# Hybrid attention block on Trainium2: branch B's output projection in strips of 256 columns with six banks for the heads, and rotary blocks whose squares have no fixed order

## The chip, the cores and the metric

The kernel runs on one core of one Trainium2 chip. The metric is the device time of one execution in microseconds. The engines are TensorE (PE; its weight loads are listed apart as PEld), VectorE (DVE), ScalarE (ACT), GpSimd (POOL) and SyncE (SP), which issues every DMA of this kernel in one queue, in order. PSUM has eight banks of 128 x 512 float32.

## The reference, cut to what matters

One layer of an encoder block over 512 tokens of width 2048, in float32:

```python
h = rmsnorm(x, norm_g)
qa, ka, va, za, qb, kb, vb, zb, ga, gb = split(h @ w_in)        # w_in: 2048 x 10752
# branch A: differential attention, 8 heads of 128 (two halves of 64)
qa, ka = apply_rope(qa), apply_rope(ka)
p  = softmax(q1 k1^T / 8) - lam * softmax(q2 k2^T / 8)
oa = rmsnorm(p @ va, subln_g) * (1 - lam_init)
ya = (oa * silu(za)) @ w_out_a                                  # 1024 x 2048
# branch B: 8 query heads, 2 key heads of 128, normalised, then axial rotary
qb = axial_rope(rmsnorm(qb, q_norm_g)); kb = axial_rope(rmsnorm(kb, k_norm_g))
ob = softmax(qb kb^T / sqrt(128)) @ vb
yb = (ob * silu(zb)) @ w_out_b                                  # 1024 x 2048
merged = sigmoid(ga) * ya + sigmoid(gb) * yb
out = rmsnorm(x + merged @ w_o, final_g)
```

## The kernel before

**Products in parts.** Each float32 operand of a large product is written as hi + lo, both in the type fp32r: `hi_lo` casts on ScalarE (L115, `w_hi<-w_raw`) and subtracts on VectorE (L116, `w_lo<-w_raw,w_hi`). Three matmuls (hi hi, hi lo, lo hi) then stand for one. Weights come in tiles of 128 x 1024 numbers (`w_raw`), eight buffers; the split tiles `w_hi`, `w_lo` have three buffers each. So the two splits of a tile run ahead of TensorE by at most two or three tiles.

**Stages.** The input is normalised and turned; then come the projections of `w_in`. The large ones use Strassen's scheme, seven products for eight (`strassen`, L197 on, whose matmuls of 256 columns are L248; the wide form has L329). The last Strassen stage is the four projections of the gates z (L654 to L667): each is a call of `strassen` with 336 matmuls of 256 columns, 24 to a weight tile. Its results pass `gate`, a SiLU on ScalarE (L659) and a store (L661). After each call some blocks of branch B's queries and keys get their norm and rotary factors.

**A rotary block** is `rope_b` (L606 to L634): a load of 128 x 512 from the scratch `pv` into `cols` (L612), four squares with row sums on ScalarE (L617), a reciprocal root on GpSimd (L111, L112 in `rsqrt_pool`), four products and sums on GpSimd (L628 twice, L629, L630), for the two key heads (numbers 8 and 9) four scalings on ScalarE (L633), and a store to `pv` (L634). `tc.keep_in_program_order` holds the squares where the program has them in ScalarE's queue. The list `to_rope` says which blocks are written behind which of the four projections. In the text below the blocks are called R1 to R10 in the order of that list: 0, 8, 1, 2, ...

**Who orders what.** A scheduler orders the instructions of every engine. In the attention stage TensorE alone follows the program's order by hand (`manual_schedule`), and the others follow the scheduler.

**Attention** has sixteen heads in the order `HEADS`: B0 B1 A0 B2 B3 A1 B4 B5 B6 A2 B7 A3 A4 A5 A6 A7. Each head makes four tiles of scores (an A head two products for each), takes the softmax, turns the four tiles of p (`turn_p`: four transposes into one bank, then the splits `ph` and `pl` out of it), and multiplies with v (`attend`, in `finish`). An A head ends with `norm`: a matmul with ones sums the squares `sqh`, `sql` of the output. PSUM banks come in two rings: `acc` for projections and `aux` for heads. Six of the eight banks are in `aux`, two in `acc`.

**Fillers.** While heads wait for their softmax, TensorE takes steps of other work: `fill(n)` takes n steps from the generator `fillers`. Each is one weight tile with its 24 or so matmuls. First come the last projections (`FILL_BLOCKS`), then, from the last A heads on, branch B's output projection yb. `FILLS` holds three digits for each head, the number of steps at its three places. In the projection, yb goes through four strips of 512 columns. A strip has four blocks of tokens at a time, so it takes four banks: before it starts, two banks go from `aux` to `acc`. When a bank is complete, `yb_done` loads the gate `gg`, multiplies on VectorE and stores to `yg`.

```python
ring = banks["aux"]
banks["acc"] += [ring.pop(0), ring.pop(0)]
...
few = len(banks["aux"]) < 6
```

So `few` is true from the head on in which yb begins, and then the turning of p is in two halves with a step between, and one step stands between the third and fourth tile of scores. The branch's head outputs are kept in SBUF or in the scratch `og` and split with `og_split` when a step needs them. After the heads come ya (L1057 on), the last product with `w_o`, and the final norm.

Of the kernel before, what the change touches and what calls it, by code (L numbers as in the profile page):

```python
# [11 lines left out]
F32 = mybir.dt.float32  # L12
F32R = mybir.dt.float32r
AF = mybir.ActivationFunctionType
ALU = mybir.AluOpType
AX = mybir.AxisListType

P = 128
D = 2048
S = 512  # L20
NT = S // P
# [30 lines left out]
def hybrid_block_kernel(  # L52
# [8 lines left out]
    nc = tc.nc  # L61
# [5 lines left out]
    banks = {}  # L67
# [10 lines left out]
    def share_banks(**kw):  # L78
        banks.update(kw)
# [10 lines left out]
    def aux(*shape):  # L90
        return bank("aux", shape or (S,))
# [284 lines left out]
    gg = dram.tile([S, 2 * D], F32, name="gg")  # L376
    og = dram.tile([2 * BW, S], F32, name="og")
    yg = dram.tile([S, D], F32, name="yg")
# [59 lines left out]
    with tc.tile_pool(name="xs", bufs=1) as xs:  # L438
# [4 lines left out]
        sq = xs.tile([P, D], F32, name="sq", tag="s4h")  # L443
        with tc.tile_pool(name="xn", bufs=1) as xn:
# [5 lines left out]
            for t in range(NT):  # L450
                for i in range(2):
                    c = slice(i * (D // 2), (i + 1) * (D // 2))
# [5 lines left out]
            ps = aux()  # L458
            nc.tensor.transpose(out=ps[:, :NK], in_=grow, identity=ident[:NK, :NK])
            nc.vector.tensor_copy(out=gn, in_=ps[:, :NK])  # L460
            for t in range(NT):
                ss = xn.tile([P, 2], F32, name="ss", tag="ss", bufs=4)
                for i in range(2):
                    c = slice(i * (D // 2), (i + 1) * (D // 2))
# [4 lines left out]
                for c in (slice(0, 512), slice(512, 1024)):  # L469
                    v = xt[:, t].rearrange("p (k c) -> p k c", k=2)[:, :, c]  # L470
# [105 lines left out]
        with tc.tile_pool(name="sp", bufs=6) as sp:  # L576
# [29 lines left out]
            def rope_b(n):  # L606


                b = B_QB + n if n < 8 else B_KB + n - 8
                assert written[b] == NT  # L610
                v = sp.tile([P, NT, P], F32, name="cols", tag="cols", bufs=2)
                nc.sync.dma_start(out=v, in_=pv[b])  # L612
                sq = sp.tile([P, P], F32, name="bsq", tag="bsq", bufs=1)
                ss = rb[:, n, :]
                for t in range(NT):
                    tc.keep_in_program_order(
                        nc.scalar.activation(out=sq, in_=v[:, t, :], func=AF.Square, accum_out=ss[:, t:t + 1]))  # L617
                if n < 8:

                    rsqrt_pool(ss, ss, 1.0, P * EPS, NT)  # L620
                else:
                    rsqrt_pool(ss, ss, 1.0 / P, EPS, NT)
                t2 = sp.tile([P, NT, P], F32, name="rope2", tag="rope2", bufs=1)
                tcb, tsb = tabs["q" if n < 8 else "k"]
                for r in range(2):
                    d, s, m = (x.rearrange("p t (a r j) -> p t a r j", r=2, j=32)[:, :, :, q, :]
                               for x, q in ((t2, r), (v, 1 - r), (tsb, r)))
                    nc.gpsimd.tensor_tensor(out=d, in0=s, in1=m, op=ALU.mult)  # L628
                nc.gpsimd.tensor_tensor(out=v, in0=v, in1=tcb, op=ALU.mult)  # L629
                nc.gpsimd.tensor_tensor(out=v, in0=v, in1=t2, op=ALU.add)  # L630
                if n >= 8:
                    for t in range(NT):
                        nc.scalar.mul(out=v[:, t, :], in_=v[:, t, :], mul=ss[:, t:t + 1])  # L633
                nc.sync.dma_start(out=pv[b], in_=v)  # L634

            b_table("q", q_norm_g)
            b_table("k", k_norm_g)
            to_rope = [(0, 8, 1), (2, 3, 4), (5, 9), (6, 7)]


            nc.sync.dma_start(out=sub_g, in_=subln_g.rearrange("o p -> p o"))
# [32 lines left out]
    at = ap.enter_context(tc.tile_pool(name="at", bufs=2))  # L674
# [221 lines left out]
    def og_tiles(half):  # L896
        ogq[half] = tuple(xa.tile([P, 8, S], F32R, name=f"og{half}{e}", tag=f"a{half + 1}{e}") for e in "hl")

    def og_act(k, t=None):
        return tuple(v[:, k % 8, :] if t is None else v[:, k % 8, t * P:t * P + P] for v in ogq[k // 8])  # L900
# [18 lines left out]
    def fill_steps(blocks, **kw):  # L919
        def place():  # L920
            return at.tile([P, S], F32, name="kq", tag="kq")

        return (plain_rows if blocks[0] < B_VA else plain_cols)(blocks, place, **kw)

    def fillers():
        for blocks in FILL_BLOCKS[:-1]:
            yield from fill_steps(blocks)

        for n, _ in enumerate(fill_steps(FILL_BLOCKS[-1], order=[8, 12, 0, 4])):
            if n == 3:  # L930
                og_tiles(1)
            og_split(3)
            yield
        og_tiles(0)

        ring = banks["aux"]
        banks["acc"] += [ring.pop(0), ring.pop(0)]
        for n in range(4):
            def yb_done(t, ps, n=n):
                rows = slice(t * P, (t + 1) * P)  # L940
                g = at.tile([P, S], F32, name="rows", tag="kq", bufs=2)
                nc.sync.dma_start(out=g, in_=gg[rows, D + n * S:D + n * S + S])
                nc.vector.tensor_tensor(out=g, in0=ps, in1=g, op=ALU.mult)
                nc.sync.dma_start(out=yg[rows, n * S:n * S + S], in_=g)

            steps = stream_steps(w_out_b, [(n * S, S)], 8, True, lambda k, t: og_act(8 + k, t), yb_done)
            for last in (10, 10, 12, 12, 14, 14, 16, 16):

                while not split_og.issuperset(range(8, last)):
                    og_split(1)  # L950
                    yield
                next(steps)
                og_split(1)
                yield

    filler = fillers()

    def fill(n):
        for _ in range(n):
            next(filler, None)  # L960


    with tc.manual_schedule(engines={mybir.EngineType.PE}):
        heads = [(HeadA if h[0] == "A" else HeadB)(int(h[1])) for h in HEADS]
        heads[0].prepare()
        heads[1].prepare()
        heads[0].double()
        fill(FILL_FIRST)
        heads[0].turn()
        fill(2)  # L970
        for n, head in enumerate(heads):
            f = [int(c) for c in FILLS[n]]
            last = heads[n - 1] if n else None
            if n + 1 < len(heads):
                heads[n + 1].double()
            few = len(banks["aux"]) < 6
            head.scores(0)
            head.scores(1)
            fill(f[0])
            if last:  # L980
                last.finish()
            head.scores(2)
            if few:
                fill(1)
            head.scores(3)
            if n + 1 < len(heads):
                heads[n + 1].turn()
            if n + 2 < len(heads):
                heads[n + 2].prepare()
            fill(f[1] - few)  # L990
            if few:
                head.turn_p((0, 1))
                fill(1)
                head.turn_p((2, 3))
            else:
                head.turn_p()
            if last:
                last.norm()
            fill(f[2] - few)
        head.finish()  # L1000
        head.norm()

# [2 lines left out]
        pass  # L1005
    og_split()
    ap.close()
    share_banks(acc=banks["acc"], aux=banks["aux"])


    mp = ctx.enter_context(tc.tile_pool(name="mp", bufs=1))
# [4 lines left out]
    with tc.tile_pool(name="ya", bufs=1) as yp:  # L1016
# [41 lines left out]
        for n in range(4):  # L1058
            rows = [None] * NT
# [9 lines left out]
            steps = stream_steps(w_out_a, [(n * 256, 256), (1024 + n * 256, 256)], 8, True, og_act, ya_done)  # L1069
# [192 lines left out]
```

## Time and profile before

| | before |
| --- | --- |
| device time, median of 3 runs | 1409.51 us (1408.02 to 1410.52) |
| the profiled execution | 1409.93 us |
| its span in the trace | 1408.2 us |
| mean granted clock of TensorE | 0.983 |
| PE busy | 1342.4 us, 95% of the span |
| PEld | 1180.6 us, 84% |
| DVE | 1079.7 us, 77% |
| ACT | 714.5 us, 51% |
| POOL | 224.1 us, 16% |

Busy times are those of one execution, taken by the profiler. Times in rows are microseconds from the start of the span, unless a row says ns. `out<-in` are the names of tiles in the program; a form such as 128x512 is partitions by elements. A granted clock of 1.0 is 2.4 GHz; it falls to 0.5, which is 1.2 GHz, and a number between is a mean over a stretch. The span ends 1.7 us below the execution's own time.

### The profile page before, as it was taken

How to read it: one execution, taken by the hardware profiler on the slowest of the kernel's cores; microseconds unless marked ns; L12 is line 12 of the kernel's file. 1: busy time of each engine (PE TensorE's matmuls, PEld its weight loads, DVE VectorE, ACT ScalarE, POOL GpSimd, SP SyncE). 2: the span in 40 equal slices, each digit the busy share in tenths (PEclk: the TensorE clock that was granted, in tenths of full speed). 3: DMA queues.
4: the chain of work that ended last, by engine and by line, in shares of the span. 5: the costliest groups of instructions: out<-in, count | busy, mean ns of one | idle time of the engine just before them, and what ended most of it. 6: DMA issues, size and time to landing. Idle time of an engine off the chain costs nothing. (4 is left out here: it accounts for less than half of the span.)

```text
span 1408.2 us, 20166 instructions
## 1 busy us (share of the span) xinstructions
PE 1342.4 (95%) x7625; PEld 1180.6 (84%) x7625; DVE 1079.7 (77%) x1271; ACT 714.5 (51%) x1104; POOL 224.1 (16%) x194
## 2 busy tenths in 40 slices
PE   6999999999999999989789899999899899999997
PEld 5998888888888888989789688888777778899997
DVE  5976877777787787868664587869888756799986
ACT  7643343444444444455344467657677643444444
POOL 1000000000000000543543411422220000004322
PEclk9999999999999999999899999999999999999999
DMA  8244654636372825535436684454554346453333
GB/s 284 81 146 134 201 173 133 211 97 232 91 253 75 269 90 179 166 112 165 150 103 174 196 245 135 135 166 153 184 163 150 112 148 211 149 207 111 103 105 120
DMA packets 174561, 222.33 MB, mean 158 GB/s; under 512 B 12016, under 2 KB 110592, under 8 KB 173824
## 3 DMA queue, kind: packets, MB, share of 16 engines
q1 hardware_dynamic: 174464, 221.04, 49.6%
q8 instruction: 60, 0.98, 0.3%
q14 instruction: 37, 0.30, 0.1%
HBM read 181.15 MB, written 35.65 MB: 154 GB/s over the span
## 5 line engine op out<-in xcount | busy, mean ns | idle before, releaser
L115 ACT CAST w_hi<-w_raw 128x1024 fp32r<-128x1024 f32 x357 | 375.0, 1052 | 474.1 <-PE acc L329 235.9
L116 DVE TENSOR_TENSOR w_lo<-w_raw,w_hi 128x1024 fp32r<-128x1024 f32 x357 | 452.4, 1271 | 189.0 <-ACT w_hi L115 186.0
L317 DVE TENSOR_TENSOR w_raw<-w_raw 128x1024 f32<-128x1024 f32 x96 | 116.8, 1222 | 23.6 <-DMA w_raw<-in_w_in_dram 22.5
L220 DVE TENSOR_TENSOR w_raw<-w_raw 128x1024 f32<-128x1024 f32 x72 | 97.7, 1357 | 0.9
L599 POOL TENSOR_TENSOR tc_q<-tc_q,g_q 128x128 f32<-128x128 f32 x4 | 4.7, 1195 | 556.8 <-DMA g_k<-in_k_norm_g_dram 556.8
L329 PE MATMUL acc<-w_hi,a2h 128*128 128x512 f32 x192 | 74.7, 389 | 0.0
L329 PE MATMUL acc<-w_hi,a2l 128*128 128x512 f32 x192 | 74.7, 389 | 0.0
L329 PE MATMUL acc<-w_lo,a2h 128*128 128x512 f32 x192 | 74.7, 389 | 0.0
L717 DVE TENSOR_REDUCE nmax<-aux 128x1 f32<-128x512 f32 x96 | 62.4, 680 | 8.3 <-PE aux L807 4.5
L186 PE MATMUL acc<-a1h,w_hi 128*128 128x512 f32 (+1 forms) x160 | 56.5, 358 | 0.2 <-ACT a1h L492 0.2
L186 PE MATMUL acc<-a2h,w_hi 128*128 128x512 f32 (+1 forms) x160 | 56.3, 355 | 0.0
L186 PE MATMUL acc<-a2l,w_hi 128*128 128x512 f32 (+1 forms) x160 | 56.0, 351 | 0.0
L186 PE MATMUL acc<-a2h,w_lo 128*128 128x512 f32 (+1 forms) x160 | 55.9, 350 | 0.0
L186 PE MATMUL acc<-a1h,w_lo 128*128 128x512 f32 (+1 forms) x160 | 55.8, 353 | 0.0
L186 PE MATMUL acc<-a1l,w_hi 128*128 128x512 f32 (+1 forms) x160 | 55.6, 353 | 0.1
L186 PE MATMUL acc<-w_hi,og1h 128*128 128x512 f32 x128 | 51.3, 401 | 0.0
L186 PE MATMUL acc<-w_lo,og1h 128*128 128x512 f32 x128 | 50.7, 396 | 0.0
L186 PE MATMUL acc<-w_hi,og1l 128*128 128x512 f32 x128 | 50.5, 394 | 0.0
L186 PE MATMUL acc<-w_hi,og0h 128*128 128x512 f32 x128 | 50.1, 392 | 0.0
L186 PE MATMUL acc<-w_hi,og0l 128*128 128x512 f32 x128 | 49.9, 390 | 0.0
L186 PE MATMUL acc<-w_lo,og0h 128*128 128x512 f32 x128 | 49.8, 389 | 0.0
L705 POOL TENSOR_TENSOR cols<-cols,ca 128x512 f32<-128x512 f32 x16 | 23.8, 1487 | 152.2 <-DMA cols<-pv 128.0
(360 smaller groups left out, 4045.3 us busy)
## 6 DMA issues: line engine op xcount, KB each, us to landing
w_raw<-in_w_in_dram SPq DMA_DIRECT2D x160, 512.0 KB, 4.5
w_raw<-in_w_in_dram SPq DMA_DIRECT2D x64, 256.0 KB, 4.2
w_raw<-in_w_o_dram SPq DMA_DIRECT2D x32, 512.0 KB, 3.5
cols<-pv SPq DMA_DIRECT2D x36, 256.0 KB, 3.7
w_raw<-in_w_out_b_dram SPq DMA_DIRECT2D x16, 512.0 KB, 4.2
w_raw<-in_w_out_a_dram SPq DMA_DIRECT2D x32, 256.0 KB, 3.6
xt<-in_x_dram SPq DMA_DIRECT2D x8, 512.0 KB, 8.0
gg<-wide_c SPq DMA_DIRECT2D x8, 512.0 KB, 3.6
```

Of the source, the lines that this page charges most:

```text
L115: nc.scalar.copy(out=hi, in_=src)
L116: nc.vector.tensor_tensor(out=lo, in0=src, in1=hi.bitcast(F32), op=ALU.subtract)
L186: nc.tensor.matmul(out=acc[b][:, place], lhsT=l, rhs=r, start=first and kc == order[0] and k == 0 and i == 0, stop=last and kc == order[-1 ...
L220: nc.vector.tensor_tensor(out=d, in0=u, in1=v, op=ALU.subtract)
L317: nc.vector.tensor_tensor(out=d, in0=u, in1=v, op=ALU.subtract)
L329: nc.tensor.matmul(out=ps[:, u, :], lhsT=l[:, kk, sl], rhs=r[:, k, :], start=kk == 0 and i == 0, stop=kk == H - 1 and i == 2)
L599: nc.gpsimd.tensor_tensor(out=tcb[:, t, :], in0=tcb[:, t, :], in1=g, op=ALU.mult)
L705: nc.gpsimd.tensor_tensor(out=v, in0=v, in1=ca, op=ALU.mult)
L717: nc.vector.tensor_reduce(out=nmax, in_=sps, axis=AX.X, op=ALU.max, negate=True)
```

## The change

It has two parts. **Rotary blocks:** `cols` gets four buffers instead of two, the squares lose their fixed place in ScalarE's queue, and the ten blocks are written behind the first three projections of z instead of all four, as 4, 3 and 3. **The projection yb:** eight strips of 256 columns instead of four of 512. Two blocks of tokens share a bank, so that a strip needs two banks, and no bank leaves the heads' ring. A step is one weight tile of 512 rows by 256 columns, two to a strip, and the gate and the product are tiles of 128 x 2 x 256. Since the ring stays at six, `few` stays false; the head's turning of p is in one piece in every head, and the earlier A head's `norm` stands before it with one step between, not behind it. At the end the two banks go to `acc` for the stage after.

```diff
@@ -608,13 +608,12 @@
 
                 b = B_QB + n if n < 8 else B_KB + n - 8
                 assert written[b] == NT
-                v = sp.tile([P, NT, P], F32, name="cols", tag="cols", bufs=2)
+                v = sp.tile([P, NT, P], F32, name="cols", tag="cols", bufs=4)
                 nc.sync.dma_start(out=v, in_=pv[b])
                 sq = sp.tile([P, P], F32, name="bsq", tag="bsq", bufs=1)
                 ss = rb[:, n, :]
                 for t in range(NT):
-                    tc.keep_in_program_order(
-                        nc.scalar.activation(out=sq, in_=v[:, t, :], func=AF.Square, accum_out=ss[:, t:t + 1]))
+                    nc.scalar.activation(out=sq, in_=v[:, t, :], func=AF.Square, accum_out=ss[:, t:t + 1])
                 if n < 8:
 
                     rsqrt_pool(ss, ss, 1.0, P * EPS, NT)
@@ -635,7 +634,7 @@
 
             b_table("q", q_norm_g)
             b_table("k", k_norm_g)
-            to_rope = [(0, 8, 1), (2, 3, 4), (5, 9), (6, 7)]
+            to_rope = [(0, 8, 1, 2), (3, 4, 5), (9, 6, 7), ()]
 
 
             nc.sync.dma_start(out=sub_g, in_=subln_g.rearrange("o p -> p o"))
@@ -932,19 +931,16 @@
             og_split(3)
             yield
         og_tiles(0)
-
-        ring = banks["aux"]
-        banks["acc"] += [ring.pop(0), ring.pop(0)]
-        for n in range(4):
+        for n in range(8):
             def yb_done(t, ps, n=n):
-                rows = slice(t * P, (t + 1) * P)
-                g = at.tile([P, S], F32, name="rows", tag="kq", bufs=2)
-                nc.sync.dma_start(out=g, in_=gg[rows, D + n * S:D + n * S + S])
-                nc.vector.tensor_tensor(out=g, in0=ps, in1=g, op=ALU.mult)
-                nc.sync.dma_start(out=yg[rows, n * S:n * S + S], in_=g)
-
-            steps = stream_steps(w_out_b, [(n * S, S)], 8, True, lambda k, t: og_act(8 + k, t), yb_done)
-            for last in (10, 10, 12, 12, 14, 14, 16, 16):
+                rows, c = slice(t * P, (t + 2) * P), n * 256
+                g = at.tile([P, 2, 256], F32, name="rows", tag="kq", bufs=2)
+                nc.sync.dma_start(out=g, in_=gg[rows, D + c:D + c + 256].rearrange("(u p) n -> p u n", p=P))
+                nc.vector.tensor_tensor(out=g, in0=ps.rearrange("p (u n) -> p u n", u=2), in1=g, op=ALU.mult)
+                nc.sync.dma_start(out=yg[rows, c:c + 256].rearrange("(u p) n -> p u n", p=P), in_=g)
+
+            steps = stream_steps(w_out_b, [(n * 256, 256)], 8, True, lambda k, t: og_act(8 + k, t), yb_done)
+            for last in (12, 12, 16, 16):
 
                 while not split_og.issuperset(range(8, last)):
                     og_split(1)
@@ -974,29 +970,31 @@
             if n + 1 < len(heads):
                 heads[n + 1].double()
             few = len(banks["aux"]) < 6
+            if few:
+                f = (1, 3, 1)
             head.scores(0)
             head.scores(1)
             fill(f[0])
             if last:
                 last.finish()
             head.scores(2)
-            if few:
-                fill(1)
+            fill(few)
             head.scores(3)
             if n + 1 < len(heads):
                 heads[n + 1].turn()
             if n + 2 < len(heads):
                 heads[n + 2].prepare()
-            fill(f[1] - few)
+            fill(f[1] - 1)
+            if last:
+                last.norm()
             if few:
                 head.turn_p((0, 1))
                 fill(1)
                 head.turn_p((2, 3))
             else:
+                fill(1)
                 head.turn_p()
-            if last:
-                last.norm()
-            fill(f[2] - few)
+            fill(f[2])
         head.finish()
         head.norm()
 
@@ -1005,7 +1003,8 @@
         pass
     og_split()
     ap.close()
-    share_banks(acc=banks["acc"], aux=banks["aux"])
+    ring = banks["aux"]
+    share_banks(acc=banks["acc"] + ring[:2], aux=ring[2:])
 
 
     mp = ctx.enter_context(tc.tile_pool(name="mp", bufs=1))
```

Four pieces of the queues follow. In rows of the changed kernel the line numbers are lower by one.

**ScalarE in the first z projection.** `L617` are the squares of a block, `L633` the scalings of a key head, `L659` a gate's SiLU. Before:

```order
L115 CAST w_hi<-w_raw 128x1024 x2
L659 ACTIVATE kept<-kept 128x512
L617 ACTIVATE bsq,rb<-cols 128x128 x4
L115 CAST w_hi<-w_raw 128x1024
L617 ACTIVATE bsq,rb<-cols 128x128 x4
L115 CAST w_hi<-w_raw 128x1024
L633 ACTIVATE cols<-cols,rb 128x128 x4
L263 COPY kept<-acc 128x512
```

And now:

```order
L115 CAST w_hi<-w_raw 128x1024 x2
L616 ACTIVATE bsq,rb<-cols 128x128
L115 CAST w_hi<-w_raw 128x1024
L616 ACTIVATE bsq,rb<-cols 128x128 x5
L115 CAST w_hi<-w_raw 128x1024
L632 ACTIVATE cols<-cols,rb 128x128 x4
L616 ACTIVATE bsq,rb<-cols 128x128 x2
L115 CAST w_hi<-w_raw 128x1024
```

The squares of four blocks and the scalings of the first key head now stand among the casts of the first projection, where before the first two blocks stood at its end.

**SyncE in the first z projection, now.** `L612` loads a block, `L633` stores one, `L214` loads weights, `L660` stores a gate.

```order
L612 DMA cols<-pv 128x512 x4
L214 DMA w_raw<-in_w_in_dram 128x4x256
L633 DMA pv<-cols 128x512
L660 DMA zg<-kept 128x2x256
L612 DMA cols<-pv 128x512
L214 DMA w_raw<-in_w_in_dram 128x4x256 x3
L633 DMA pv<-cols 128x512
L214 DMA w_raw<-in_w_in_dram 128x4x256
L633 DMA pv<-cols 128x512
L214 DMA w_raw<-in_w_in_dram 128x4x256
L633 DMA pv<-cols 128x512
L612 DMA cols<-pv 128x512
```

Four loads of blocks stand in a row at the start; from the fifth on a load stands behind stores of earlier blocks.

**SyncE where attention begins.** `L141` loads weights of the last projections, `L680` the tables of branch A, `L690` the first blocks of q, k and v. Before:

```order
L661 DMA zg<-kept 128x2x256
L141 DMA w_raw<-in_w_in_dram 128x4x128 x2
L634 DMA pv<-cols 128x512 x2
L141 DMA w_raw<-in_w_in_dram 128x4x128
L680 DMA ca<-in_cos_a_dram 128x512
L680 DMA sa<-in_sin_a_dram 128x512
L690 DMA cols<-pv 128x512 x3
L690 DMA vb<-pv 128x512
```

And now:

```order
L660 DMA zg<-kept 128x2x256
L141 DMA w_raw<-in_w_in_dram 128x4x128 x2
L679 DMA ca<-in_cos_a_dram 128x512
L679 DMA sa<-in_sin_a_dram 128x512
L689 DMA cols<-pv 128x512 x3
L689 DMA vb<-pv 128x512
```

The two stores of rotary blocks ahead of attention's loads stand there no more.

**VectorE in an A head beside yb.** `pl` is the split of a turned p, `y` the chain of an earlier head's norm, `rows` the gate's product of yb, `nmax` the maximum of a tile of scores. Before:

```order
L116 TENSOR_TENSOR pl<-aux,ph 128x512 x2
L116 TENSOR_TENSOR w_lo<-w_raw,w_hi 128x1024
L116 TENSOR_TENSOR pl<-aux,ph 128x512 x2
L717 TENSOR_REDUCE nmax<-aux 128x1
L839 SCALAR_TENSOR_TENSOR y_9507<-aux,y_9507 128x512
L717 TENSOR_REDUCE nmax<-aux 128x1
L840 SCALAR_TENSOR_TENSOR y_9507<-y_9507,y_9504 128x512
L717 TENSOR_REDUCE nmax<-aux 128x1
L841 SCALAR_TENSOR_TENSOR y_9507<-o,sub_g,y_9507 128x512
```

And now:

```order
L116 TENSOR_TENSOR w_lo<-w_raw,w_hi 128x1024
L838 SCALAR_TENSOR_TENSOR y_9559<-aux,y_9559 128x512
L939 TENSOR_TENSOR rows<-acc,rows 128x512
L839 SCALAR_TENSOR_TENSOR y_9559<-y_9559,y_9556 128x512
L116 TENSOR_TENSOR pl<-aux,ph 128x512
L840 SCALAR_TENSOR_TENSOR y_9559<-o,sub_g,y_9559 128x512
L116 TENSOR_TENSOR pl<-aux,ph 128x512 x2
L116 TENSOR_TENSOR og0l<-rows,og0h 128x512
L116 TENSOR_TENSOR pl<-aux,ph 128x512
L939 TENSOR_TENSOR rows<-acc,rows 128x512
L716 TENSOR_REDUCE nmax<-aux 128x1 x4
```

The weight split between the two pairs of `pl` is gone from there; the norm's chain and the gate's product now stand around the four `pl` and ahead of the scores' maxima.

## Rows read from the trace of the kernel before

**Rows 1.** The chain that ended last: start us, length us, engine, line, instructions.

```profile
1175.25 21.82 PE acc L186 x96
1296.17 83.14 PE acc L248 x691
```

**Rows 2.** Busy time by stretch (z projections, attention's start, A heads beside yb).

```profile
core 0: us, PE busy (x) PEld busy (x) DVE busy (x) ACT busy (x) POOL busy (x), PEclk, DMA share, GB/s
570.90:759.50 188.60, 170.26 (x1345) 168.77 (x1346) 133.34 (x118) 85.25 (x150) 80.75 (x74) 0.94 0.48 148
...
775.60:800.00 24.40, 17.90 (x76) 14.72 (x75) 10.55 (x18) 9.80 (x18) 8.56 (x6) 0.86 0.80 233
...
991.40:1143.50 152.10, 139.96 (x628) 113.04 (x627) 121.35 (x199) 101.57 (x195) 22.45 (x15) 0.96 0.45 144
```

**Rows 3.** TensorE's waits, whole kernel: waited for, us in total, times, longest us.

```profile
PE acc L248 <- ACT w_hi L115: 16.4, 3, 7.0
...
PE aux L806 <- DVE pl L116: 6.5, 3, 4.2
PE aux L728 <- DMA vb<-pv: 6.5, 1, 6.5
...
PE aux L831 <- ACT sqh L115: 0.8, 1, 0.8
```

**Rows 4.** ScalarE in time, 560 to 700: start, length; in brackets idle before, and releaser.

```profile
613.30 0.31 ACT L617 ACTIVATE bsq<-cols 128x128 f32<-128x128 f32 x1
613.73 0.31 ACT L617 ACTIVATE bsq<-cols 128x128 f32<-128x128 f32 x1
...
627.81 1.27 ACT L633 ACTIVATE cols<-cols,rb 128x128 f32<-128x128 f32 x4 [9.65 <-POOL cols L630]
...
681.53 0.31 ACT L617 ACTIVATE bsq<-cols 128x128 f32<-128x128 f32 x1 [11.94 <-DMA cols<-pv]
```

**Rows 5.** GpSimd in time, 560 to 800; columns as in rows 4.

```profile
597.07 1.43 POOL L628 TENSOR_TENSOR rope<-cols,ts_q 128x256 f32<-128x256 f32 x2
...
688.29 3.26 POOL L628 TENSOR_TENSOR rope<-cols,ts_q 128x256 f32<-128x256 f32 x2
...
714.71 0.99 POOL L111 TENSOR_SCALAR rb<-rb 128x4 f32<-128x4 f32 x1 [23.15 <-ACT bsq L617]
...
718.92 1.70 POOL L630 TENSOR_TENSOR cols<-cols,rope 128x512 f32<-128x512 f32 x1
```

**Rows 6.** GpSimd by tile, 570 to 780: ns shortest/median/longest, first and last start.

```profile
L628 POOL TENSOR_TENSOR rope<-cols,ts_q x16: 717/740/1723, 597.1 to 767.4; 128x256 f32<-128x256 f32 x16
L630 POOL TENSOR_TENSOR cols<-cols,rope x10: 1261/1431/2285, 618.9 to 771.7; 128x512 f32<-128x512 f32 x10
L629 POOL TENSOR_TENSOR cols<-cols,tc_q x8: 1272/1731/2197, 615.7 to 769.5; 128x512 f32<-128x512 f32 x8
L111 POOL TENSOR_SCALAR rb<-rb x10: 194/194/1053, 614.7 to 769.2; 128x4 f32<-128x4 f32 x10
L112 POOL TENSOR_TENSOR rb<-rb,neg_half x10: 1001/1017/1997, 617.9 to 770.7; 128x4 f32<-128x4 f32 x10
```

**Rows 7.** The page: two groups (busy us, mean ns | idle before); DMA (KB, us to landing).

```profile
L115 ACT CAST w_hi<-w_raw 128x1024 fp32r<-128x1024 f32 x357 | 375.0, 1052 | 474.1 <-PE acc L329 235.9
L116 DVE TENSOR_TENSOR w_lo<-w_raw,w_hi 128x1024 fp32r<-128x1024 f32 x357 | 452.4, 1271 | 189.0 <-ACT w_hi L115 186.0
...
cols<-pv SPq DMA_DIRECT2D x36, 256.0 KB, 3.7
```

**Rows 8.** SyncE's queue in time, 530 to 800; columns as in rows 4.

```profile
579.97 0.90 SPq L612 DMA_DIRECT2D cols<-pv  x2
...
766.63 7.72 SPq L634 DMA_DIRECT2D pv<-cols  x2
...
778.43 0.43 SPq L690 DMA_DIRECT2D vb<-pv  x1
```

**Rows 9.** Groups by line and form: busy us, mean ns of one | idle before.

```profile
L248 PEld LDWEIGHTS acc<-w_hi,s1h 128*128 128x128 f32 x80 | 15.4, 192 | 0.0
```

## The prediction

> **What bounds the kernel now.** I read the table of busy time by stage first, then TensorE's waits, then each waiting place engine by engine in order of time. TensorE is busy 95% of the span, so only two things count: its own work, and the time in which it stands or runs at half clock.
>
> Its pace comes from the chain of work that ended last, where nothing interrupts it: 96 matmuls of 512 columns in 21.82 us are 0.2273 us each, and 691 of 256 columns in 83.14 us are 0.1203 us each [rows 1].
>
> Three stretches lose time [rows 2]. The four z projections run from 570.9 to 759.5; their 4 x 336 = 1344 matmuls of 256 columns would take 161.7 us and take 188.6, so **26.9 us** are lost: 16.4 are three waits for w_hi [rows 3], most of the rest is the granted clock, 0.94 on average (2.4 GHz falling to 1.2 after each long wait). Where attention begins, TensorE waits 6.5 us for a load of vb [rows 3], and the clock is 0.86 over those 24.4 us. In the A heads that share TensorE with branch B's projection (991.4 to 1143.5) it is idle for 152.10 - 139.96 = 12.1 us, and a clock of 0.96 costs about 0.04 x 152 = 6.1 more: **18.2 us**. The largest item there is 6.5 us of scores waiting for a PSUM bank that VectorE still reads as pl [rows 3].
>
> **The rotary blocks.** I number the ten blocks R1 to R10 in their order; R2 and R8 are the key heads, whose four scalings on ScalarE wait for GpSimd's end. The waits for w_hi come from ScalarE standing in line: 9.65 us before R2's scalings, because GpSimd ends R2 only then, and 11.94 us before a block's squares, because its load comes late [rows 4]. A cast of w_hi (1.05 us) behind such a wait is what TensorE lacks. The change removes neither kind. The order of ScalarE shows all ten blocks inside the first two z projections, with R2's scalings after ten casts of the first one. I follow them with the rows' durations.
>
> GpSimd starts R1 at 597.1 [rows 5], since the tables before it do not move. A block has six operations: twice L628, L111, L629, L112, L630. Their shortest times sum to 5.2 us, their medians to 5.9, their longest to 11.0 [rows 6]. The fifth query block took 3.26 + (720.6 - 714.7) = 9.2 us while VectorE was busy [rows 5]. I take 5.2 where VectorE stands and up to 8.6 where it works.
> - R1 ends at 602.3, R2 at 607.5. ScalarE's tenth and eleventh casts lie around the scalings; the eleventh tile of the first projection would be due at 570.9 + 11 x 2.88 = 602.6 (24 matmuls of 0.1203 a tile). Scalings 1.3, two squares of 0.43 each, cast 1.05 [rows 4, 7]: w_hi at 610.7, w_lo (1.27) at 612.0. Stall: 9.4 us.
> - On SyncE the load of R6 stands behind the store of R4, since four buffers carry it. R3 and R4 at 6.8 each end at 621.1; the load lands 3.7 us later [rows 7], three squares and the cast follow: w_lo of the second projection's first tile at 628.9, while TensorE has ended the first at 623.2 (570.9, 14 tiles of 2.88, the 9.4, and 2.5 lost at half clock). Stall: 5.7.
> - R7's and R8's squares wait in the same way; about 1.2 each, 2.4.
> - R8 ends at 649 (R5 5.2, R6 8.6, R7 7.4, R8 6.7); its scalings, a square and the cast give w_lo at 653.1 where 648.8 is due (five tiles later, the 2.4, and 3.1 at half clock). Stall: 4.3.
>
> That is 21.8 us of stalls. Now 26.9 - 16.4 = 10.5 go to clock and small waits with three long waits; with three again I add 8 to 9: about 30. The third and fourth projections are then free of rotary work and lose nothing. **Net +3.1**, from -8 (each block 1 us faster and no wait for loads) to +21 (the first rival). Forty squares and eight scalings are the same work as before, and the two more buffers cost nothing: the first four loads are issued in a row from 580.0 on, where two are now [rows 8], and the first is wanted at 584.
>
> **The start of attention.** Now SyncE holds the loads for attention behind two stores of rotary blocks, at 766.6 to 774.4; vb is issued at 778.4 [rows 8]. Those stores are gone from there, and only the last pair of weight loads and the last gate's store, at about 764, are ahead. vb would land near 770, some 5 us before it is wanted. The wait of 6.5 goes, and with it the half clock that follows: 0.14 x 24.4 = 3.4, of which about 1 lies inside the wait. **Net -8.8**, from -9.9 to 0.
>
> **The projection in 256 columns.** 384 matmuls of 512 columns become 768 of 256: 768 x 0.1203 - 384 x 0.2273 = 92.4 - 87.3 = **+5.1 us**, all on the path.
>
> The Trainium skill (TensorE: Matmul & The Clock Gate, Back-to-back issue gap) gives N / 2.4 + 2.5 ns for a warm matmul, so 109.2 and 215.8 ns. By that the step would cost an estimated 1.0 us instead of 5.1. The rows are 10% slower at 256 columns and 5% at 512, so the trace decides.
>
> What it buys: heads keep six banks in the ring. In the ring's order the scores after a turned head then meet banks whose pl is read two steps earlier, and no weight split stands between the four pl on VectorE. So the waits for pl, for the earlier head's output and for y go. What is left: a strip of 256 columns has only two banks, and the next strip's first step needs the first of them one step (24 x 0.1203 = 2.9 us) after it closed. Between come the wait for VectorE and one multiplication. Eight strips fall so that in three places both steps are adjacent: in the first A head, where VectorE is behind by 3 us now, I take 3 us, at the two others 1 each: 5 us stay of 18.2. Bounds: 1, and three waits as long as the longest today, 4.2 each [rows 3], with 1 more: 13.6. **Net -13.2 + 5.1 = -8.1**, from -12 to +0.5. Loads and stores of gates and products are as many and as large as before; their lines are half as long, and a load is issued two steps ahead of its use.
>
> **Norms earlier.** Three norms in the B heads now follow their head's output by one step. The nearest row is the last norm, which follows by about as much and waits 0.8 us for ScalarE [rows 3]: 0 to 2.4, **+1.2**.
>
> **Sum.** The profiled execution took 1409.93 us (median of the runs 1409.51, so the same). 1409.93 + 3.1 - 8.8 - 8.1 + 1.2 = **1397.3 us**.
>
> **Rivals.**
> - GpSimd sets the pace, and slower than I take it. All blocks at 9.2 instead of a mean of 6.5 make R8 end 8 x 2.7 = 21.3 later: **1418.6**, slower than before. It decides from a mean of 8.1. For it: the time of the fifth query block. Against: VectorE stands while TensorE stalls, and then blocks take 5.2.
> - Two banks cost what six give: 13.6 instead of 5 stay, **1405.9**. For it: VectorE is busy 121 of 152 us there [rows 2]. Against: the multiplications stand early in its order.
> - Attention still starts late, for another load or cast: **1406.1**. Against: every store that stood ahead is gone.
> - Squares wait for no load, only the scalings stall: 5.7 + 2.4 + 2.9 for the clock less, **1386.3**. For it: loads are issued as buffers free. Against: SyncE's order has R6's load behind R4's store.
> - Weight loads show. 384 more loads of 192 ns [rows 9], none hidden: some 74 us more, **1471**. Against: 691 matmuls with 691 loads ran at 0.1203 each, shorter than a load. The Trainium skill (same page, The mechanism) says that a weight load overlaps running matmuls only where it uses another row group, or the background weight buffer; that first half speaks for this rival, and the trace does not agree with it.
>
> **How the numbers follow.** Forecast 0.51, in 1390 to 1404; GpSimd's pace 0.08; two banks 0.15; late attention 0.08; no wait for loads 0.10; weight loads 0.01; things that I don't see 0.07. A measurement of this kernel can tell about 0.2% (2.8 us) from no change: faster is below 1406.7, slower above 1412.3. The forecast and the gain without load waits are faster; two banks and late attention lie at the edge, two thirds of them faster; the unseen is split evenly. Faster 0.79, same 0.12, slower 0.09. The range that leaves out 2 in 10 takes the case below, with its bound, and the edge cases, not GpSimd's pace: 1384 to 1409.
>
> **What would show it.** In the trace of after: one wait of 8 to 10 us for w_hi near 603, a second near 624, a third near 650, none after 660; ScalarE idle before R2's scalings until about 607.5; a z stage of 188 to 196 us; no wait for vb; the A-head stretch 143 to 145 us with at most one wait of 3 us for the multiplications. Wrong would make it: R8's end later than 662, a wait where attention starts, or waits for the multiplications at most strips.

## The result, and the profile after

The changed kernel takes **1396.0 us** (median of three runs, 1394.5 to 1396.9) against 1409.5 before: a ratio of 0.9904, interval 0.9882 to 0.9926. 1397.3 was predicted. Its profiled span is 1394.2 us, 14.0 less than before.

Busy time by stretch, cut at the same places of the program as [rows 2] (the first row is the z projections, the third attention's start behind them, the fifth the A heads beside yb; columns as there):

```profile
570.80:764.40 193.60, 173.68 (x1345) 170.98 (x1346) 129.75 (x118) 88.12 (x167) 85.81 (x84) 0.94 0.47 147
764.40:780.50 16.10, 16.10 (x72) 13.28 (x71) 5.06 (x5) 5.41 (x6) 1.13 (x1) 1.00 0.93 274
780.50:796.00 15.50, 15.50 (x75) 12.92 (x74) 9.32 (x18) 9.68 (x17) 8.99 (x8) 1.00 0.61 181
796.00:986.20 190.20, 187.77 (x918) 155.79 (x916) 152.74 (x273) 128.81 (x255) 51.00 (x33) 0.99 0.56 166
986.20:1129.60 143.40, 140.63 (x1014) 132.92 (x1013) 120.24 (x205) 100.48 (x198) 20.36 (x15) 0.99 0.50 156
```

The z projections are 5.0 us longer (193.6 for 188.6). Attention's start is 8.9 shorter: 15.5 at full clock for 24.4 at 0.86. The heads between are 1.2 shorter, and the A heads beside yb 8.7 (143.4 for 152.1). The rest of the program is the same to 0.3 us. TensorE's waits after, the whole kernel, answer to [rows 3]:

```profile
PE acc L248 <- ACT w_hi L115: 14.5, 5, 5.1
...
PE acc L248 <- DVE w_lo L116: 5.5, 7, 1.3
...
PE aux L831 <- DVE sql L116: 2.2, 1, 2.2
PE acc L186 <- DVE rows L939: 2.0, 1, 2.0
...
PE aux L805 <- DVE pl L116: 0.7, 2, 0.5
```

The wait for vb is gone, that for pl is 0.7 instead of 6.5, and a strip of 256 columns waits once, 2.0 us, for a multiplication (L939). ScalarE in the z projections (columns as in [rows 4]):

```profile
587.24 0.31 ACT L616 ACTIVATE bsq<-cols 128x128 f32<-128x128 f32 x1 [3.23 <-DMA cols<-pv]
...
607.25 1.28 ACT L632 ACTIVATE cols<-cols,rb 128x128 f32<-128x128 f32 x4 [7.09 <-POOL cols L629]
...
625.06 0.31 ACT L616 ACTIVATE bsq<-cols 128x128 f32<-128x128 f32 x1 [9.41 <-DMA cols<-pv]
...
651.31 1.28 ACT L632 ACTIVATE cols<-cols,rb 128x128 f32<-128x128 f32 x4 [6.17 <-POOL cols L629]
```

R2's scalings start at 607.25 (607.5 was worked out), R6's squares wait for their load, R8's scalings start at 651.31 (649). Those three places are as predicted. The first row is not: R1's squares stand before two loads of ScalarE's function tables (1.28 us each) and the next casts, and their load is late. GpSimd starts R1 (`rope`) at 592.95, 4.1 us earlier than before [rows 5], since its tables take less time; the last of them, before and then changed:

```profile
592.85 4.26 POOL L602 TENSOR_TENSOR ts_k<-ts_k,g_k 128x64 f32<-128x64 f32 x8
```

```profile
590.72 2.27 POOL L602 TENSOR_TENSOR ts_k<-ts_k,g_k 128x64 f32<-128x64 f32 x8
592.95 2.41 POOL L627 TENSOR_TENSOR rope<-cols,ts_q 128x256 f32<-128x256 f32 x2
```

To tell the parts apart, this table gives the time between the same matmuls in each kernel's trace: the start of the z projections; the first matmul behind them; the first turned p of attention; B7's product with v; the first transpose of the stage ya. It is worked out from the starts of those matmuls.

| kernel | z | to the first turned p | to B7's product | to ya |
| --- | --- | --- | --- | --- |
| before | 188.5 | 45.7 | 193.9 | 174.3 |
| changed | 193.4 | 36.8 | 194.1 | 164.3 |
| e_rope_only | 193.7 | 36.8 | 194.5 | 175.2 |
| e_yb_only | 188.4 | 45.2 | 196.1 | 161.5 |
| e_four_banks | 193.4 | 36.8 | 194.7 | 164.0 |
| e_no_gap | 193.4 | 36.8 | 196.1 | 174.5 |
| e_before_step | 187.9 | 45.0 | 193.7 | 169.1 |
| e_512_spread | 193.9 | 36.8 | 192.6 | 165.8 |
| e_norm_late | 193.7 | 36.8 | 193.7 | 167.2 |
| e_bufs6 | 196.7 | 36.8 | 194.6 | 165.0 |
| e_bufs6_pool | 203.2 | 36.8 | 193.9 | 161.6 |
| e_store_pool6 | 184.3 | 36.8 | 195.6 | 164.9 |
| e_store_pool6_norm | 183.9 | 36.8 | 195.6 | 163.9 |
| e_store_pool6_kept | 182.8 | 36.8 | 195.1 | 162.6 |

The third and fourth columns move by about 2 us from one profiled execution to the next: in e_no_gap and the changed kernel TensorE, VectorE, ScalarE and GpSimd have the same order of work until 1008 us, beyond the third column, and it differs by 2.0. So single differences of that size in these columns decide nothing.

### The profile page after: what moved, and what is told of

It reads as the page before. It is cut to its first block, busy times and chain, and to the rows that moved or that the text cites. A ratio compares the mean times of both kernels' runs of the same rounds, so it can differ in the third digit from the quotient of the medians.

```text
span 1394.2 us, 20919 instructions
## 1 busy us (share of the span) xinstructions
PE 1344.5 (96%) x8009; PEld 1200.2 (86%) x8009; DVE 1069.6 (77%) x1271; ACT 711.1 (51%) x1104; POOL 218.0 (16%) x194
## 4 chain that ended last, share of the span: by engine, by line
PE 80%; DVE 6%; POOL 5%; DMA 3%; ACT 3%; issue 3%; SPq 0%; POOLq 0%; DVEq 0%; ACTq 0%
PE acc L329 32%; PE acc L186 21%; PE acc L248 19%; PE aux L762 2%; DVE w_lo L116 2%; PE aux L749 1%; PE aux L875 1%; DMA cols<-pv 1%; POOL rope L627 1%; POOL cols L628 1%; PE aux L805 1%; PE aux L806 1%; POOL cols L629 1%; DMA w_raw<-in_w_in_dram 1%; DMA xt<-in_x_dram 1%
## 5 line engine op out<-in xcount | busy, mean ns | idle before, releaser
L317 DVE TENSOR_TENSOR w_raw<-w_raw 128x1024 f32<-128x1024 f32 x96 | 116.8, 1222 | 23.3 <-DMA w_raw<-in_w_in_dram 22.1
L220 DVE TENSOR_TENSOR w_raw<-w_raw 128x1024 f32<-128x1024 f32 x72 | 94.7, 1315 | 3.4 <-DMA w_raw<-in_w_in_dram 2.5
L186 PE MATMUL acc<-w_hi,og1h 128*128 128x256 f32 x256 | 73.5, 287 | 2.0 <-DVE rows L939 2.0
L186 PE MATMUL acc<-w_hi,og1l 128*128 128x256 f32 x256 | 73.2, 286 | 0.0
L186 PE MATMUL acc<-w_lo,og1h 128*128 128x256 f32 x256 | 73.1, 286 | 0.0
L186 PEld LDWEIGHTS acc<-w_hi,og1h 128*128 128x128 f32 x256 | 49.7, 194 | 2.8 <-DVE rows L939 2.2
L186 PEld LDWEIGHTS acc<-w_lo,og1h 128*128 128x128 f32 x256 | 49.7, 194 | 0.6
```

The source lines that it names most:

```text
L186: nc.tensor.matmul(out=acc[b][:, place], lhsT=l, rhs=r, start=first and kc == order[0] and k == 0 and i == 0, stop=last and kc == order[-1 ...
L220: nc.vector.tensor_tensor(out=d, in0=u, in1=v, op=ALU.subtract)
L317: nc.vector.tensor_tensor(out=d, in0=u, in1=v, op=ALU.subtract)
```

## The experiments

### The two parts apart

```diff
# e_rope_only, against the kernel before
-v = sp.tile([P, NT, P], F32, name="cols", tag="cols", bufs=2)
+v = sp.tile([P, NT, P], F32, name="cols", tag="cols", bufs=4)
-tc.keep_in_program_order(nc.scalar.activation(out=sq, in_=v[:, t, :], func=AF.Square, accum_out=ss[:, t:t + 1]))
+nc.scalar.activation(out=sq, in_=v[:, t, :], func=AF.Square, accum_out=ss[:, t:t + 1])
-to_rope = [(0, 8, 1), (2, 3, 4), (5, 9), (6, 7)]
+to_rope = [(0, 8, 1, 2), (3, 4, 5), (9, 6, 7), ()]
# e_yb_only: the changed kernel with these three lines as before
```

> The kernel before with the rotary part of the change alone (four buffers, squares without an order, the new list). Theory: the two parts add up. The traces give +4.9 us for the z projections and -8.9 us where attention starts, so about 1405.5 us against 1409.5 before; no wait of TensorE for vb. Rival: the start of attention gains only because the heads keep six banks; then the rotary part alone costs about 4.9 and takes some 1414 us.

Measured: 1407.3 us, ratio 0.9976 (0.9966 to 0.9985). The z projections lose 5.2 us and attention's start gains 8.9, with the heads at four banks: the start's gain is the rotary part's own. Its trace has no wait for vb.

> The changed kernel with the rotary part undone: strips of 256 columns, six banks for the heads, norms earlier. Theory: -8.9 us in the A heads and -0.9 in the B heads, so about 1399.7 us, with the 6.5 us wait for vb back. Rival: part of what the A heads gain comes from loads that the earlier start of attention moves forward; then the gain is under 6 us, above 1403.5.

Measured: 1397.7 us, ratio 0.9911 (0.9897 to 0.9924). The A heads gain without any change at attention's start, where a wait is back (5.6 us, for a load of `cols`). The parts add up to 15 us where the change as a whole gains 13.5; the intervals cover that.

### What makes the A heads faster

```diff
# e_four_banks, against the changed kernel
 og_tiles(0)
+ring = banks["aux"]
+banks["acc"] += [ring.pop(0), ring.pop(0)]
 for n in range(8):
...
-share_banks(acc=banks["acc"] + ring[:2], aux=ring[2:])
+share_banks(acc=banks["acc"], aux=banks["aux"])
```

> The changed kernel, but two banks go from the heads' ring to the projection before the first strip, as in the kernel before; the strips stay at 256 columns. Theory: 256 columns cost 5 us by themselves and the six banks bring 13; without them the A heads lose about 13 us, 1409 us. Rival: the shorter steps or the earlier norms bring the gain; then the time stays within 3 us of 1396. The four banks of the projection should take away its one wait of 2.0 us for a multiplication.

Measured: 1395.1 us, ratio 0.9891 (0.9876 to 0.9906). The theory fell. With four banks the A heads take 164.0 us, with six 164.3, and the waits for pl are as short:

```profile
PE aux L805 <- DVE pl L116: 1.1, 2, 0.6
```

So the six banks are not needed to take the waits away. The run changes more than the banks, though: with four of them `few` is true, so p is turned in two halves with a step between, and one step stands between the third and fourth tile of scores. Four banks with p turned in one piece were not run. What the changed head loop has in both cases, and the one before has not, beside the short strips and the earlier norm, is a step of the projection between the turning of p and the next head's scores. Before, `few` took that step away (`f[2] - few` is 0) and put one between the third and fourth tile of scores.

```diff
# e_no_gap, against the changed kernel
-                fill(1)
+                fill(1 + f[2])
                 head.turn_p()
-            fill(f[2])
# e_before_step, against the kernel before
-            fill(f[0])
+            fill(f[0] - few)
...
-            fill(f[2] - few)
+            fill(f[2])
```

> The changed kernel with six banks, but in the A heads beside the projection the step behind the turning of p goes ahead of it, so that the next head's scores follow the turning at once. Theory of the step: scores wait for pl again, 1 to 2 us in each of five heads and half clock behind the longer ones, 1401 to 1406 us. Rival (the prediction's): six banks are enough, since the scores meet banks that were read before; within 2 us of 1396.

Measured: 1408.9 us, ratio 0.9991 (0.9980 to 1.0002). That is above both ranges: one step in another place, with six banks as they are, gives the whole gain of the A heads back (174.5 us; 174.3 before). TensorE's waits in its A heads, and VectorE in the second of them:

```profile
PE aux L805 <- DVE pl L116: 9.9, 6, 5.4
```

```profile
1047.35 2.48 DVE L116 TENSOR_TENSOR pl<-aux,ph 128x512 fp32r<-128x512 f32 x4
```

That is more than the 6.5 of [rows 3], with two banks more and with the four pl in a row, no weight split between them.

> The kernel before with one edit: in the heads beside the projection one step of it moves from ahead of the earlier head's product with v to behind the norm, between the turning of p and the next scores. Strips of 512 columns, four banks, norm and rotary blocks as before. Theory of the step: the waits for pl (6.5 us) and for the earlier head's output (2.9) go with most of the half clock, 6 to 11 us less, 1399 to 1404. Rival: the earlier norm or the banks are needed; 1407 or more.

Measured: 1404.0 us, ratio 0.9957 (0.9942 to 0.9973). The step alone, with 512 columns, four banks and everything else as before, takes 5.2 us out of the A heads. Its waits there:

```profile
PE acc L186 <- DVE rows L943: 3.4, 2, 2.6
PE aux L806 <- DVE rows L887: 2.8, 1, 2.8
PE aux L831 <- ACT sqh L115: 1.6, 1, 1.6
PE aux L750 <- DVE p L815: 1.6, 1, 1.6
```

The waits for pl are gone, and that for the earlier head's output (L887), which the theory had going too, stays; waits for VectorE's multiplications (L943, `rows` of yb) have come.

```diff
# e_512_spread: the changed kernel with the strips of the kernel before
-for n in range(8):
+ring = banks["aux"]
+banks["acc"] += [ring.pop(0), ring.pop(0)]
+for n in range(4):
...
```

Not shown are `yb_done`, the limits of `og_split` and `share_banks`, which are also those of the kernel before.

> The changed kernel with the projection of the kernel before: strips of 512 columns, four banks for them, four for the heads. What stays of the change there is where the steps and the norm stand in an A head: one step between the turning of p and the next head's scores, the norm ahead of the turning. New theory, after the run with four banks took as long as that with six: it is this step that took the waits away, and 256 columns cost 5 us for nothing; then 5 us less than that run, about 1390 us. Rival: short strips are needed too, because a strip of 512 columns closes its banks in a burst; then 1395 or more.

Measured: 1398.6 us, ratio 0.9919 (0.9903 to 0.9935), so the rival held: 512 columns are not better. Their A heads take 165.8 us, 1.8 more than with 256 columns on four banks. These waits stand there:

```profile
PE aux L749 <- DVE y L838: 2.2, 3, 1.3
PE acc L186 <- DVE rows L941: 2.1, 2, 2.0
PE aux L805 <- DVE pl L116: 1.1, 2, 0.6
PE aux L762 <- ACT p L719: 0.9, 2, 0.6
```

The 256 columns do cost about what was worked out: in the next rows (TensorE in time, changed and before) 20 matmuls of 256 take 2.39 us from start to start, 0.1195 each, and 19 of 512 take 4.31, 0.2268 each.

```profile
1010.42 0.28 PE L186 MATMUL acc<-w_hi,og1h 128*128 128x256 f32 x1
...
1012.81 0.28 PE L186 MATMUL acc<-w_hi,og1l 128*128 128x256 f32 x1
```

```profile
1022.53 0.39 PE L186 MATMUL acc<-w_hi,og1h 128*128 128x512 f32 x1
...
1026.84 0.39 PE L186 MATMUL acc<-w_lo,og1h 128*128 128x512 f32 x1
```

768 of the one less 384 of the other are 4.7 us (the two decimals of the rows leave some 0.4 either way). The shorter strips get most of it back in waits: in these heads TensorE waits 6.3 us by the four lines above, and 3.0 in e_four_banks; the granted clock is 0.99 and 1.00. The Trainium skill (TensorE: Matmul & The Clock Gate, Back-to-back issue gap) gives 0.1092 and 0.2158 for a single warm matmul, by which the difference would be an estimated 1.0 us; this trace does not agree.

```diff
# e_norm_late, against the changed kernel
 fill(f[1] - 1)
-if last:
-    last.norm()
...
     head.turn_p()
+if last:
+    last.norm()
 fill(f[2])
```

> The changed kernel with the earlier head's norm behind the turning of p again, as in the kernel before. Theory: norms earlier cost one wait of 2.2 us for the split of the squares, in the first A head, and the half clock behind it; with the norm later that wait goes and the time is 2 to 4 us less, about 1393. Rival: the norm's chain on VectorE then stands behind the splits of p and the scores wait for it, 1397 to 1400.

Measured: 1397.6 us, ratio 0.9911 (0.9898 to 0.9925), which can't be told from the changed kernel's 0.9904. In the trace the wait of 2.2 us for the split squares goes, and others of the same size come, in the heads around the start of yb:

```profile
PE aux L749 <- DVE p L712: 2.9, 2, 1.5
PE acc L186 <- ACT og1h L115: 2.7, 1, 2.7
PE aux L830 <- ACT sqh L115: 1.5, 1, 1.5
```

### What the z projections wait for

```diff
# e_bufs6, against the changed kernel
-... name="cols", tag="cols", bufs=4)
+... name="cols", tag="cols", bufs=6)
# e_bufs6_pool: that, and
-nc.scalar.mul(out=v[:, t, :], in_=v[:, t, :], mul=ss[:, t:t + 1])
+nc.gpsimd.tensor_scalar(out=v[:, t, :], in0=v[:, t, :], scalar1=ss[:, t:t + 1], scalar2=None, op0=ALU.mult)
```

> The changed kernel with six buffers for rotary blocks and nothing else. Theory of the prediction: the wait at 622 us (5.4 us) is a load that stands in SyncE's queue behind the store of the fourth block; with six buffers that load stands ahead, the wait and its half clock go, and the time is 6 to 9 us less, 1387 to 1390. Rival, after the run with six buffers and scalings on GpSimd: weight loads behind the same stores then come late and take the wait's place; 1393 or more.

Measured: 1397.2 us, ratio 0.9906 (0.9889 to 0.9922): no gain. The rival's time came, but not its cause. The wait of ScalarE for R6's load is gone (one of 5.0 us for R8's is left), but with its squares done early the next thing in ScalarE's line comes sooner, and that is R8's scalings, which still wait for GpSimd. ScalarE's waits there, and TensorE's for w_hi:

```profile
ACT cols L632 <- POOL cols L629: 22.7, 2, 14.8
...
ACT bsq L616 <- DMA cols<-pv: 7.5, 2, 5.0
```

```profile
PE acc L248 <- ACT w_hi L115: 17.1, 4, 11.3
```

ScalarE waits 14.8 us before R8's scalings, where the changed kernel has 6.17. GpSimd sets the pace, and the load had only stood ahead of it.

> The changed kernel with the two causes of ScalarE's waits taken away: six buffers for rotary blocks, so that loads don't stand behind the stores of the block before last, and the key heads' scalings on GpSimd. Theory: the waits of TensorE at 607 (4.3 us), 622 (5.4) and 650 (5.3) go with the half clock behind them; the first one, at 591, stays; the z projections take 172 to 176 us instead of 193.6 and the whole 1375 to 1379. Rival: GpSimd and VectorE are short of time in themselves, and casts or w_lo come late without these two; a gain under 8 us.

Measured: 1405.9 us, ratio 0.9967 (0.9953 to 0.9981), 10 us slower than the changed kernel. Neither theory nor rival had this. TensorE waits 21.6 us in one piece at 617. That wait, then VectorE and SyncE in time around it:

```profile
PE acc L248 <- DVE w_lo L116: 26.9, 7, 21.6
```

```profile
635.83 1.79 DVE L220 TENSOR_TENSOR w_raw<-w_raw 128x1024 f32<-128x1024 f32 x1 [19.64 <-DMA w_raw<-in_w_in_dram]
```

```profile
612.75 7.45 SPq L633 DMA_DIRECT2D pv<-cols  x2
620.29 0.99 SPq L214 DMA_DIRECT2D w_raw<-in_w_in_dram  x2
625.17 5.64 SPq L633 DMA_DIRECT2D pv<-cols  x2
630.90 0.39 SPq L660 DMA_DIRECT2D zg<-kept  x1
631.38 0.45 SPq L214 DMA_DIRECT2D w_raw<-in_w_in_dram  x1
```

VectorE waits for a weight load. In SyncE's queue it stands behind stores of rotary blocks (L633), and those wait for GpSimd.

```diff
# e_store_pool6: as e_bufs6_pool, and
-nc.sync.dma_start(out=pv[b], in_=v)
+nc.gpsimd.dma_start(out=pv[b], in_=v)
```

> As the run with six buffers and the scalings on GpSimd (1405.9 us), but GpSimd issues the stores of the rotary blocks itself, so that nothing in SyncE's queue waits for GpSimd's work. Theory: the wait of 21.9 us there was a weight load behind two such stores; it goes, and with it the waits at 607, 622 and 650 of the changed kernel, z projections 168 to 176 us, 1372 to 1380 in all. Rival: loads of blocks that wait for a buffer hold the weight loads in the same queue as well; waits of over 5 us stay, above 1388.

Measured: **1387.9 us**, ratio 0.9841 (0.9826 to 0.9856). The z projections take 184.3 us, 19 less than in e_bufs6_pool by that one line. The wait of 21.6 us is gone, and those at 607 and 650; at 614 TensorE waits 7.3 us for w_hi, longer than any one wait there in the changed kernel (5.1). So the theory's 1372 to 1380 did not come; the rival's wait did, with the time at its bound. Loads that wait for a buffer still stand in SyncE's queue, and ScalarE waits for them:

```profile
PE acc L248 <- ACT w_hi L115: 9.8, 3, 7.3
...
ACT bsq L616 <- DMA cols<-pv: 21.8, 5, 9.2
```

The Trainium skill (SBUF — State Buffer, SBUF: two separate sides) warns that a DMA issued by GpSimd can starve while VectorE runs an operation in a two-port mode. No such delay shows here: the ten stores landed 2.4 us after their issue, against 2.1 for the same ten from SyncE's queue in the changed kernel (DMA issues of the two profiles). Whether VectorE ran such operations meanwhile, the trace does not say.

```profile
pv<-cols POOLq DMA_DIRECT2D x10, 256.0 KB, 2.4
```

```profile
pv<-cols SPq DMA_DIRECT2D x10, 256.0 KB, 2.1
```

```diff
# e_store_pool6_norm: that, and in the heads
-fill(f[1] - 1)
+fill(f[1] - (f[1] > 2))
 last.norm()
-fill(1)
+fill(f[1] > 2)
 head.turn_p()
```

> The same as the run with stores by GpSimd, and in the heads with two steps at the second place the earlier head's norm stands behind both instead of between them. Theory: the wait of 2.2 us for the split of the squares in the last B head and the half clock behind it go, 3 to 4 us less than that run. Rival: VectorE is behind there in any case, and the wait moves to the turning of p or to the scores; within 1.5 us of it.

Measured: 1387.4 us, ratio 0.9839 (0.9821 to 0.9858): the same. The rival held. The wait for the split squares goes and scores wait for the norm's chain in its place:

```profile
PE aux L875 <- DVE y L838: 2.3, 1, 2.3
...
PE aux L805 <- DVE y L838: 2.0, 1, 2.0
```

```diff
# e_store_pool6_kept: as e_store_pool6, and
-nc.scalar.activation(out=sq, in_=v[:, t, :], func=AF.Square, accum_out=ss[:, t:t + 1])
+tc.keep_in_program_order(nc.scalar.activation(out=sq, in_=v[:, t, :], func=AF.Square, accum_out=ss[:, t:t + 1]))
```

> The run with six buffers, scalings and stores on GpSimd (1387.9 us), with one edit: the squares keep the program's order in ScalarE's queue, as in the kernel before, so that they stand behind the casts of each projection and not between its first ones. Theory: what is left of lost time in its z projections (184.5 us where 161.7 are work) is ScalarE waiting for loads of blocks (21.8 us) with casts behind it; squares that stand later find their loads landed, z projections 166 to 172 us, 1370 to 1376 in all. Rival: blocks that start later free their buffers later, the last block's load in SyncE's queue waits for the fourth block's store and holds the next weight loads; a wait of over 5 us takes the place, above 1383.

Measured: **1384.8 us**, ratio 0.9816 (0.9803 to 0.9829), the lowest median of all, though its interval overlaps that of e_store_pool6. The rival held, in time and in cause; of the theory one part came. No square waits for a load, and the z projections take 182.8 us instead of 166 to 172. TensorE has one long wait left in the z projections instead of several, at 652. TensorE's waits, then SyncE in time:

```profile
PE acc L248 <- ACT w_hi L115: 11.4, 1, 11.4
```

```profile
624.48 22.56 SPq L612 DMA_DIRECT2D cols<-pv  x3
...
653.87 0.32 SPq L612 DMA_DIRECT2D cols<-pv  x1
654.28 4.98 SPq L214 DMA_DIRECT2D w_raw<-in_w_in_dram  x6
```

The last block's load waits for a buffer until 653.9 and holds six weight loads, as the rival said. Where that load would have to stand was not tried.

## Why the prediction was right, and where it was not

- **The sum** was 1397.3 and the median is 1396.0. Step by step, in the profiled executions, by the stretches above: z projections +3.1 predicted, +5.0 measured; attention's start -8.8 and -8.9; norms and the A heads together -6.9 and -9.9, of which 1.2 lie ahead of the first scores beside yb.
- **The z projections**: three places came as worked out from GpSimd's pace, R2's scalings at 607.25 for 607.5, R8's at 651.31 for 649, the stall near 622 by R6's load. That the times fit so closely is luck, since two errors cancel. GpSimd began R1 at 592.95, where 597.1 was said "since the tables before it do not move"; and its eight blocks took 7.3 us on average, where 6.5 was taken (R1 8.0 for 5.2). So the rival of a slower GpSimd was in part true (its 8 x 2.7 is 21.6, not 21.3, which changes nothing). What was missed is the first stall. R1's squares, free of an order, went ahead of casts of w_hi and of two table loads (1.28 us each) and waited 3.23 us for their own load. So the predicted stall of 9.4 at 603 came as two smaller ones, at 591 and 607. The rival without load waits is out for this kernel. e_bufs6 shows that it would have paid nothing: behind the load stands GpSimd.
- **Attention's start** was right in cause and size. e_rope_only shows it alone.
- **The A heads**: the size was right (-8.7 for -8.1) and the reason wrong, so the size was luck. The step that failed is "What it buys: heads keep six banks in the ring". In e_four_banks the ring has four banks in these heads and the time is the same; in e_no_gap it has six, no weight split stands between the four pl, and all is lost: neither of the two reasons given is enough. It is the step of the projection between turned p and the next scores, which gives VectorE time to read pl out of the banks. The order of TensorE's work showed that move, and I had put its effect down to the ring. That step alone gives 5.2 of the 10.0 us; how the rest is shared between the earlier norm, the shorter strips and the phase of the heads was not told apart, since these differ by 1 to 3 us each.
- **256 columns** cost 4.7 us of TensorE's time where 5.1 was said. That they cost nothing in the end, since TensorE waits more beside strips of 512 columns (e_512_spread), was not in the prediction.
- **Norms earlier**: +1.2 was said, with waits of 0 to 2.4 us. One wait of 2.2 came, and waits of the same size went. e_norm_late and e_store_pool6_norm can't tell the sum from nothing.
- **Weight loads** did not show: matmuls of 0.1195 us ran with a load each, while a load lasts 0.19 [rows 9].

## What to carry to other kernels

Where scores wait for a bank that is still being read, put other work between before giving the ring more banks: one step was worth 5 us in the A heads when added alone (e_before_step) and 10 when taken away (e_no_gap; some 13 in all, of which 2 lie ahead of anything that the edit moves). Six banks in place of four, with p turned in one piece in place of halves, were worth nothing (1396.0 and 1395.1). A queue that takes its DMAs in order must not hold stores that wait for a slow engine ahead of loads that a fast one needs; let the engine that ends the work issue its store, which took 18 us off here beside six buffers and scalings on GpSimd (e_store_pool6 against e_bufs6_pool). When a wait is removed, look in the same line for what comes next, which in the z projections was each time something that waited for GpSimd.

## What the runs showed of the hardware

The same four scalings of 128 x 128 on GpSimd took 2.35 us once and 4.87 another time in one kernel (e_store_pool6, GpSimd in time, both key heads). The busy times of those two stretches (columns as in [rows 2]) show what differs:

```profile
611.28 2.35 POOL L632 TENSOR_SCALAR cols<-cols,rb 128x128 f32<-128x128 f32 x4
...
666.32 4.87 POOL L632 TENSOR_SCALAR cols<-cols,rb 128x128 f32<-128x128 f32 x4
```

```profile
611.28:613.63 2.35, 2.35 (x20) 2.16 (x19) 0.00 (x0) 0.00 (x0) 2.35 (x5) 1.00 1.09 360
666.32:671.19 4.87, 4.87 (x43) 4.87 (x43) 4.53 (x5) 2.63 (x3) 4.87 (x5) 1.00 0.73 232
```

VectorE stood still in the first and was busy for 4.53 us in the second: a factor of two without any change in the work. It is no fixed factor, since in the same trace products of 128 x 256 took 0.74 us beside a busy VectorE once and 1.59 another time; which of VectorE's operations slow GpSimd these runs do not show. Issuing a store cost GpSimd 0.61 to 0.78 us each.
